# An early product moved into the first full chunk pair, a fifth buffer for cast weights in place of one for raw blocks, and token-sum stores on GpSimd's queue

## The chip, the cores and the metric

The kernel runs on one core of a Trainium2 chip. It is one program on five engines with a queue of instructions each: TensorE (PE, matrix products), VectorE (DVE), ScalarE (ACT), GpSimd (POOL) and SyncE (SP), which here only issues DMAs. An engine works through its queue in order and waits on semaphores where an instruction needs another engine's result. Copies between device memory and on-chip memory are issued from the queues of SP, POOL and, at a few places, ACT.

The metric is the device time in microseconds of one execution. Before the change it is 956.69 us, the median of 3 runs (956.43, 956.69, 957.40). The profile comes from one further execution.

## The reference

One layer on 1024 tokens of width 1024 with 16 learned meta tokens ahead. All weights and data are float32.

```python
u = rmsnorm(h, g_pre_mix[l])
z = u @ w_in[l]
q, k, v, xr, yr = jnp.split(z, split_at, axis=-1)
attn = sliding_window_attention_with_sinks(q, k, v, attn_sinks[l])
xr = causal_depthwise_conv(xr, conv_w[l], conv_b[l])
hr = rg_lru(xr, w_a[l], b_a[l], w_x[l], b_x[l], lru_lambda[l])
rec = gelu(yr) * hr
mix = concatenate([attn, rec]) @ w_out[l]
h = h + rmsnorm(mix, g_post_mix[l])
u = rmsnorm(h, g_pre_ffn[l])
f = square(relu(u @ w_ff1[l])) @ w_ff2[l]
h = h + rmsnorm(f, g_post_ffn[l])
return h[:, N_META:]
```

(The reshapes are left out.) The change mostly concerns the feed-forward part, `u @ w_ff1` (1024 to 4096, called FFN1 here) and the product with `w_ff2` (4096 to 1024, FFN2).

## The kernel before

**Precision.** A float32 operand is used as two parts. ACT casts it to a "high" part (L96), DVE subtracts that from the source and leaves a "low" part (L99); `split` issues both. A product is then three matmuls per slice, in `mm3`: high times high (L125), high times low (L126), low times high (L127). `product` calls `mm3` four times, which is twelve matmuls of 128x128 by 128x512.

**Fewer products.** Both FFN matrices and the tokens are cut into quarters, and sums and differences of quarters are multiplied, so that seven products do what eight would do plainly. FFN1 works on 16 chunks p of 256 columns of `w_ff1`. The token operands are called b11 and b21 (first half of the tokens), ot2 and ot3 (sums and differences, `t_sums`), ot1, ob22, ob21 and ot4.

- First the *early products*: `p1(p)` is a weight block times b11, `p2(p)` a weight block times b21, for chunks 0 to 3. `p2` accumulates into a bank "pt" and DVE adds the bank to block "11" (L1106). In the program text they come as p1(0), p1(1), p2(0), p2(1), the sums, p1(2), p1(3), p2(2), p2(3).
- *Stage A* (loop at L1171, p = 0 to 15): product of chunk p's first weight sum with ot2 into the bank `ya[p]`, a copy of that bank into block "12" by ACT (L1177), then `p1(p+2)`, then the product with ot3 into the same bank, and a second copy (L1181). For chunks 0 and 1 no `p1(p+2)` is left, because these were early.
- *Stage B* (`p5`, ob22, L1194 to L1214) reads one of the weight sums back from device memory.
- *Stage C* (L1299 to L1321) multiplies by ob21 and ot4. The parts of ot4 are read back from device memory, `t4_dram`, by four DMAs (L1220), and the first product on them is laid out by parts (`product_by_parts`, L1222 to L1229).
- *FFN2* (L1441 to L1468) has 7 sums i times 8 steps q. A step takes 24 matmuls.

**Weights of a chunk.** `prep_a(p)` loads two blocks of 512 KB, r0 and r1, from SP's queue. DVE builds four sums or differences in place (`combine`, L992). Two of them are split into a pair of weight buffers and one into a small pair `hl`. The last sum stays in r1 and is stored to `s_dram` from POOL's queue (L1037).

**Token sums for ot4.** `t_rest` forms them during chunks 3 to 8 of stage A, splits them, and stores four parts of 512 KB to `t4_dram` from SP's queue (L1168).

**FFN2's weights.** `fetch_2(n)` loads one or two blocks of 512 KB for step n into tags "raw" and "e" in turn; where a sum of two blocks is wanted, some steps let the second load accumulate onto the first from POOL's queue (L1261), and the others take two loads (L1264) that DVE combines in `prep_2` (L1273). Then the block is split into weight buffers (L1279).

**Buffers.** All big tiles are 4 KB per partition and come from one slab, by tag, with a fixed number of buffers each: "raw" 2, "ws" 4, "a" 16, "b" 17, "c" 8, "d" 4, "e" 3. "ws" holds cast weights (a pair takes two), "raw" and "e" hold raw blocks. In attention the key tile km sits in an "e" buffer. A new tile waits until the tile that had its buffer before has been read for the last time; this is how a buffer decides when a load or a cast can go.

**Order.** A scheduler lays the program out on the engines' queues by its own estimate of the times, so that instructions of neighbouring steps mix. `behind(name, ins)` fixes an order without a wait: ins must stand after the named instruction. `last_mm[0]` holds the name of the last matmul that `mm3` issued; `w_lows[n]` the low part of step n's weights.

Of the kernel before, what the change touches and what calls it, by code (L numbers as in the profile page):

```python
# [10 lines left out]
F32R = mybir.dt.float32r  # L11
# [5 lines left out]
P = 128  # L17
# [20 lines left out]
def hybrid_layer(  # L38
# [6 lines left out]
    nc = tc.nc  # L45
# [6 lines left out]
    ps = ctx.enter_context(tc.tile_pool(name="ps", bufs=2, space=PSUM))  # L52
    dpool = ctx.enter_context(tc.tile_pool(name="dpool", bufs=1, space=DRAM))

    bufs = {"raw": 2, "ws": 4, "a": 16, "b": 17, "c": 8, "d": 4, "e": 3}
    uid = [0]

    def slot(tag, shape, dt=F32):
        uid[0] += 1
        return slab.tile(shape, dt, tag=tag, name=f"{tag}{uid[0]}", bufs=bufs[tag])  # L60

    def pair(tag, shape):
        return slot(tag, shape, F32R), slot(tag, shape, F32R)

    def bank(tag, shape=(P, 512)):
        uid[0] += 1
        return ps.tile(list(shape), F32, tag=tag, name=f"ps_{tag}{uid[0]}")

    def f32(ap):
        return ap.bitcast(F32)  # L70
# [23 lines left out]
    def split(hi, lo, src, eng=None):  # L94
        if eng is None:
            nc.scalar.copy(hi, src)  # L96
        else:
            eng.tensor_copy(hi, src)
        low = nc.vector.tensor_tensor(lo, src, f32(hi), op=ALU.subtract).ins  # L99
        mark[0] = low.name  # L100
        return low
# [4 lines left out]
    def behind(name, *inss):  # L106
        for ins in inss:
            tc.add_manual_dep(
                ins, name,
                mybir.DependencyInfo(  # L110
                    mybir.DependencyClass.NoSync, mybir.DependencyReason.DATA
                ),
                reason="order",
            )
# [5 lines left out]
        ).ins  # L120
        return high, low

    def mm3(dst, lhs, rhs, start, stop):
        (lh, ll), (rh, rl) = lhs, rhs
        nc.tensor.matmul(dst, lh, rh, start=start, stop=False, skip_group_check=True)  # L125
        nc.tensor.matmul(dst, lh, rl, start=False, stop=False, skip_group_check=True)  # L126
        last_mm[0] = nc.tensor.matmul(  # L127
            dst, ll, rh, start=False, stop=stop, skip_group_check=True
        ).ins.name

    last_mm = [None]
# [129 lines left out]
    def project(w, pieces, sink):  # L261
        wh, wl = w
        for t0, n in pieces:
            acc = bank("acc")
            for kc in range(KC):
                uh, ul = u[kc]
                mm3(
                    acc[:, :n], (wh[:, kc, :], wl[:, kc, :]),
                    (uh[:, t0 : t0 + n], ul[:, t0 : t0 + n]),
                    kc == 0, kc == KC - 1,  # L270
                )
            sink(acc[:, :n], t0, n)
# [70 lines left out]
    def low_w(w, raw):  # L343
        chained(1, nc.vector.tensor_tensor(w[1], raw, f32(w[0]), op=ALU.subtract).ins)
# [58 lines left out]
    low_w(wv, rv)  # L403
    wq = high_w(rq)
    low_w(wq, rq)
    km = slot("e", [P, 4, 2 * P], F32R)
    nc.gpsimd.memset(f32(km[:, 0:2, 0 : P - NMETA]), 0.0)
    nc.gpsimd.memset(f32(km[:, 2:4, :]), 0.0)
    nsink = const.tile([P, 8], F32, name="nsink")
# [84 lines left out]
    for b in range(4):  # L494
# [3 lines left out]
        if b == 0:  # L498

            acc = [bank("acc"), bank("acc")]  # L500
# [11 lines left out]
            for w, (t0, n), sink, tag in (  # L512
                (wq, (16, 256), sink_q0, "o"), (wx, piece, sink_x0, "acc"),
            ):
                acc = bank(tag)
# [397 lines left out]
    t4_dram = dpool.tile([P, 2, 4, 512], F32, name="t4_dram")  # L913
# [73 lines left out]
    def w1_load(dst, b, p, a0, a1):  # L987
        c0 = 256 * p
        nc.sync.dma_start(dst, w1v[b][:, :, c0 + P * a0 : c0 + P * a1])

    def combine(dst, x0, x1, op):
        return nc.vector.tensor_tensor(dst, x0, x1, op=op).ins  # L992

    def operand(tiles):
        pairs = []
        for t_ in tiles:
            hi, lo = pair("b", [P, 2, 512])
            split(hi, lo, t_)
            pairs.append((hi, lo))
        return pairs  # L1000

    def product(acc, w, op, first):
        wh, wl = w
        for kc in range(4):
            hh, ll = op[kc // 2]
            mm3(
                acc, (wh[:, kc, :], wl[:, kc, :]), (hh[:, kc % 2, :], ll[:, kc % 2, :]),
                first and kc == 0, kc == 3,
            )

    LO, HI = slice(0, P), slice(P, 2 * P)
# [3 lines left out]
    def prep_a(p, late=None):  # L1015
        r0 = slot("raw", [P, 4, 256])
        w1_load(r0, 0, p, 0, 2)
        r1 = slot("a" if 2 <= p < 6 else "d", [P, 4, 256])
        w1_load(r1, 1, p, 0, 2)
        a11, a21, a12, a22 = r0[:, :, LO], r0[:, :, HI], r1[:, :, LO], r1[:, :, HI]  # L1020
        sums = [
            combine(a22, a21, a22, ALU.add), combine(a21, a11, a21, ALU.subtract)
        ]
        if late:
            behind(late, *sums)
        hi, lo = pair("ws", [P, 4, 256])
        if p in a11_early:
            split(hi[:, :, HI], lo[:, :, HI], a21)
            first = a11_early[p]
        else:  # L1030
            split(hi, lo, r0)
            first = hi[:, :, LO], lo[:, :, LO]
        combine(a11, a22, a11, ALU.subtract)
        hl = slot("e", [P, 2, 4, P], F32R)
        split(hl[:, 0], hl[:, 1], a11)
        combine(a12, a12, a11, ALU.subtract)
        nc.gpsimd.dma_start(s_dram[p], r1)  # L1037
        return first, (hl[:, 0], hl[:, 1]), (hi[:, :, HI], lo[:, :, HI])


    def early(b, p0, hl):
        raw = slot("raw", [P, 2, 4, P])
        for k in range(2):
            w1_load(raw[:, k], b, p0 + k, 0, 1)
        split(*hl, raw)
        return {p0 + k: (hl[0][:, k], hl[1][:, k]) for k in range(2)}

    a11_early, a12_early = {}, {}

    def fetch_b(p):  # L1050
        r1 = slot(("e", "raw")[p % 2], [P, 4, 256])
        nc.sync.dma_start(r1, s_dram[p])
        return r1
# [24 lines left out]
    def block(k, p):  # L1078
        q = p // 2
        if fb[k][q] is None:  # L1080
            fb[k][q] = slot(FTAG[k][q], [P, 2, 512])
        return fb[k][q][:, p % 2, :]
# [15 lines left out]
    def p1(p, w):  # L1098
        ya[p] = bank(("acc", "s")[p // 2 % 2])
        product(ya[p], w, b11, True)  # L1100
        nc.scalar.copy(block("11", p), ya[p])

    def p2(p, w):
        y2 = bank("pt")
        product(y2, w, b21, True)
        nc.vector.tensor_tensor(block("11", p), y2, block("11", p), op=ALU.add)  # L1106

    for t in range(8):
# [12 lines left out]
        if t == 6:  # L1121
            b21 = operand(u2f[0][2:4])
            hl = slot("b", ESH, F32R), slot("e", ESH, F32R)
# [4 lines left out]
    for p in range(2):  # L1128
        p2(p, a12_early[p])
# [10 lines left out]

    t_sums(slice(0, 3 * P))
    wa[0] = prep_a(0)
    u2_tiles(7, xns[7])
    t_sums(slice(3 * P, 4 * P))
# [1 line left out]
    for p in range(2, 4):  # L1146
        p1(p, a11_early[p])
    a12_early.update(early(1, 2, pair("a", ESH)))
    for p in range(2, 4):
        p2(p, a12_early[p])  # L1150
    ot3 = [pair("b", [P, 2, 512]) for _ in range(2)]
    for i in range(2):
        behind(urgent, split(*ot3[i], t3[i]))
# [3 lines left out]
    def t_rest(k):  # L1157
        i = k % 2
        if k < 2:
            behind(mark[0], combine(u2f[1][i], u2f[1][i], u2f[0][i], ALU.subtract))  # L1160
        elif k < 4:
            behind(mark[0], combine(t2[i], u2f[0][2 + i], t2[i], ALU.subtract))
        else:
            hl = pair("a", [P, 2, 512])
            late = mark[0]
            behind(late, split(*hl, t2[i]))
            for n in range(2):
                nc.sync.dma_start(t4_dram[:, n, 2 * i : 2 * i + 2, :], f32(hl[n]))  # L1168

    raw_b, raw_c = {}, {}  # L1170
    for p in range(16):  # L1171
        if p + 2 < 16:
            wa[p + 2] = prep_a(p + 2, None if p else urgent)
        if p >= 13:
            raw_b[p - 13] = fetch_b(p - 13)
        product(ya[p], wa[p][1], ot2, False)
        nc.scalar.copy(block("12", p), ya[p])  # L1177
        if 4 <= p + 2 < 16:
            p1(p + 2, wa[p + 2][0])
        product(ya[p], wa[p][2], ot3, False)  # L1180
        nc.scalar.copy(block("21", p), ya[p])  # L1181
        if 3 <= p < 9:
            t_rest(p - 3)

        if p == 14:
            ot1 = operand(u2f[1][0:2])
# [81 lines left out]
    def prep_2(n, tag="ws"):  # L1268
        i, q = steps[n]
        fx, wx, _ = PLAN[i]  # L1270
        raws = raw_2.pop(n)
        if len(raws) == 2:
            ins = combine(raws[0], raws[0], raws[1], wx[2])  # L1273
            if i == 6:
                behind(w_low[0], ins)
            elif i > 2:
                behind(w_lows[n - 2], ins)
        wh, wl = pair(tag, [P, 2, 512])
        w_low[0] = w_lows[n] = split(wh, wl, raws[0]).name  # L1279
        if len(fx) == 3:  # L1280
            f = slot("b", [P, 2, 512])
            combine(f, fb[fx[0]][q], fb[fx[1]][q], fx[2])
        else:
            f = fb[fx[0]][q]
        fh, fl = pair("b", [P, 2, 512])
        split(fh, fl, f)
        return fh, fl, wh, wl
# [11 lines left out]
    for n, p in enumerate(third):  # L1299
# [8 lines left out]
        if p not in a12_early:  # L1308
            y2 = bank(("acc", "s")[p % 2])
# [195 lines left out]
```

## Time and profile before

| | |
|---|---|
| median of 3 runs | 956.69 us (956.43 to 957.40) |
| the profiled execution | 955.87 us |
| its span in the trace | 954.1 us |
| granted TensorE clock, mean | 0.999 |
| early products (p1 and p2 of chunks 2 and 3 at their end) | end at about 343.5 us |
| stages A, B, C | about 343.5 to 640 us |
| FFN2 | about 640 to 948 us |

Times in the trace count from the start of the span; 1.77 us of the execution's time lie outside of it. In rows of the timeline the columns are: start, length, engine, line, operation, tile written and tiles read, sizes, number of instructions merged into the row, and in brackets the idle time before it with the instruction that ended it. Successive matmuls overlap: a row of 0.39 us is followed by the next one 0.23 us later. In the rows of a tile the three numbers are the least, median and greatest length of one instruction in ns. In the table of DMA issues the last number is the median time in us from issue to landing. PEld is the loading of weights into TensorE, SPq and POOLq are the issue of DMAs in the queues of SP and POOL.

### The profile page before, as it was taken

How to read it: one execution, taken by the hardware profiler on the slowest of the kernel's cores; microseconds unless marked ns; L12 is line 12 of the kernel's file. 1: busy time of each engine (PE TensorE's matmuls, PEld its weight loads, DVE VectorE, ACT ScalarE, POOL GpSimd, SP SyncE). 2: the span in 40 equal slices, each digit the busy share in tenths (PEclk: the TensorE clock that was granted, in tenths of full speed). 3: DMA queues.
4: the chain of work that ended last, by engine and by line, in shares of the span. 5: the costliest groups of instructions: out<-in, count | busy, mean ns of one | idle time of the engine just before them, and what ended most of it. 6: DMA issues, size and time to landing. Idle time of an engine off the chain costs nothing.

```text
span 954.1 us, 12400 instructions
## 1 busy us (share of the span) xinstructions
PE 944.0 (99%) x4728; PEld 789.3 (83%) x4728; DVE 657.8 (69%) x845; ACT 504.2 (53%) x854; POOL 125.4 (13%) x184
## 2 busy tenths in 40 slices
PE   9999999999999999999999999999999999999997
PEld 8999999877888877888888878888888888888885
DVE  6567987779866776665644465477567676779893
ACT  8537766478645554443555575663533343446441
POOL 4103564320020100000000000001111000001201
PEclk9999999999999999999999999999999999999999
DMA  8221011104225366675522354325677665537924
GB/s 273 56 67 24 23 45 46 45 23 140 81 110 177 133 220 199 198 257 162 208 100 89 111 180 129 111 88 151 164 190 172 192 210 178 197 134 196 244 45 89
DMA packets 88200, 130.21 MB, mean 136 GB/s; under 512 B 13703, under 2 KB 52631, under 8 KB 88141
## 3 DMA queue, kind: packets, MB, share of 16 engines
q1 hardware_dynamic: 79548, 106.54, 33.5%
q0 software_dynamic: 8160, 21.57, 10.8%
q10 hardware_dynamic: 432, 1.31, 0.4%
q8 instruction: 37, 0.61, 0.2%
q14 instruction: 23, 0.18, 0.1%
HBM read 109.93 MB, written 18.87 MB: 135 GB/s over the span
## 4 chain that ended last, share of the span: by engine, by line
PE 94%; DVE 2%; ACT 1%; POOL 1%; DMA 1%; issue 0%; DVEq 0%; SPq 0%; POOLq 0%; ACTq 0%
PE ps_acc L125 11%; PE ps_acc L126 11%; PE ps_acc L127 11%; PE ps_pt L125 7%; PE ps_pt L126 7%; PE ps_pt L127 7%; PE ps_s L125 6%; PE ps_s L127 6%; PE ps_s L126 6%; PE ps_o L127 5%; PE ps_o L125 5%; PE ps_o L126 5%; PE ps_o L687 1%; PE ps_acc L278 1%; DMA b<-t_dram 1%; POOL c L676 1%
## 5 line engine op out<-in xcount | busy, mean ns | idle before, releaser
L96 ACT CAST ws<-raw 128x1024 fp32r<-128x1024 f32 (+1 forms) x68 | 69.6, 1024 | 124.1 <-PE ps_o L126 49.4
L99 DVE TENSOR_TENSOR ws<-raw,ws 128x1024 fp32r<-128x1024 f32 (+1 forms) x69 | 82.4, 1194 | 61.7 <-ACT ws L96 60.6
L125 PE MATMUL ps_acc<-a,ws 128*128 128x256 f32 (+2 forms) x256 | 85.8, 335 | 0.0
L126 PE MATMUL ps_acc<-a,ws 128*128 128x256 f32 (+2 forms) x256 | 85.2, 333 | 0.0
L127 PE MATMUL ps_acc<-a,ws 128*128 128x256 f32 (+2 forms) x256 | 85.2, 333 | 0.0
L99 DVE TENSOR_TENSOR b<-b,b 128x1024 fp32r<-128x1024 f32 (+2 forms) x50 | 58.9, 1177 | 29.0 <-PE ps_o L126 20.1
L96 ACT CAST ws<-e 128x1024 fp32r<-128x1024 f32 x41 | 42.9, 1047 | 65.4 <-PE ps_o L126 42.1
L96 ACT CAST b<-b 128x1024 fp32r<-128x1024 f32 (+2 forms) x49 | 50.0, 1020 | 39.9 <-DVE b L992 34.4
L99 DVE TENSOR_TENSOR ws<-e,ws 128x1024 fp32r<-128x1024 f32 x41 | 50.1, 1222 | 22.1 <-ACT ws L96 22.1
L676 POOL TENSOR_SCALAR_AFFINE_SELECT c<-c 128x512 fp32r<-128x512 f32 x64 | 51.9, 831 | 70.4 <-ACT c L96 60.9
L125 PEld LDWEIGHTS ps_acc<-a,ws 128*128 128x128 f32 x256 | 48.3, 189 | 4.6 <-issue 0.2
L127 PEld LDWEIGHTS ps_acc<-a,ws 128*128 128x128 f32 x256 | 48.2, 188 | 4.5
L126 PEld LDWEIGHTS ps_acc<-a,ws 128*128 128x128 f32 x256 | 48.1, 188 | 4.5 <-issue 0.4
L125 PE MATMUL ps_acc<-ws,b 128*128 128x512 f32 (+1 forms) x120 | 46.2, 386 | 0.0
L127 PE MATMUL ps_acc<-ws,b 128*128 128x512 f32 (+1 forms) x120 | 46.2, 385 | 0.0
L126 PE MATMUL ps_acc<-ws,b 128*128 128x512 f32 (+1 forms) x120 | 46.1, 384 | 0.0
L125 PE MATMUL ps_pt<-ws,b 128*128 128x512 f32 x112 | 44.4, 396 | 0.0
L126 PE MATMUL ps_pt<-ws,b 128*128 128x512 f32 x112 | 44.1, 394 | 0.0
L127 PE MATMUL ps_pt<-ws,b 128*128 128x512 f32 x112 | 44.0, 393 | 0.0
L125 PE MATMUL ps_s<-ws,b 128*128 128x512 f32 x110 | 43.4, 395 | 0.0
L127 PE MATMUL ps_s<-ws,b 128*128 128x512 f32 x110 | 43.3, 394 | 0.0
L126 PE MATMUL ps_s<-ws,b 128*128 128x512 f32 x110 | 43.3, 393 | 0.0
(414 smaller groups left out, 2660.9 us busy)
## 6 DMA issues: line engine op xcount, KB each, us to landing
raw<-in_w_ff_dram SPq DMA_DIRECT2D x61, 512.0 KB, 4.8
e<-in_w_ff_dram SPq DMA_DIRECT2D x45, 512.0 KB, 3.5
d<-in_w_ff_dram SPq DMA_DIRECT2D x12, 512.0 KB
s_dram<-d POOLq DMA_DIRECT2D x12, 512.0 KB, 4.1
c<-in_x_dram SPq DMA_DIRECT2D x8, 512.0 KB, 3.4
raw<-in_w_in_dram SPq DMA_DIRECT2D x8, 512.0 KB
d<-in_x_dram SPq DMA_DIRECT2D x8, 512.0 KB, 3.3
out_dram<-raw SPq DMA_DIRECT2D x8, 512.0 KB
```

What stands on the lines that cost most here:

```text
L96: nc.scalar.copy(hi, src)
L99: low = nc.vector.tensor_tensor(lo, src, f32(hi), op=ALU.subtract).ins
L125: nc.tensor.matmul(dst, lh, rh, start=start, stop=False, skip_group_check=True)
L126: nc.tensor.matmul(dst, lh, rl, start=False, stop=False, skip_group_check=True)
L127: last_mm[0] = nc.tensor.matmul(dst, ll, rh, start=False, stop=stop, skip_group_check=True).ins.name
L278: last_mm[0] = nc.tensor.matmul(acc[:, :n], w[k // 2][:, kc, :], u[kc][k % 2][:, t0 : t0 + n], start=k == 0 and kc == 0, stop=k == last an ...
L676: nc.gpsimd.affine_select(out=p_[:, :, s], in_=f32(p_[:, :, 0]), pattern=[[0, 4], [g, P]], compare_op=op, fill=0.0, base=0, channel_multip ...
L687: nc.tensor.matmul(po[:, oc : oc + n], v, p_[:, pc : pc + n], start=first and k == 0, stop=last and k == 1, skip_group_check=True,)
```

## The change

It has five parts.

1. `p2(3)`, the last early product, is taken out of its place before ot3 and stands in stage A's loop at p = 0, between the copy at L1177 and the product with ot3. Its first matmul must stand behind the last one of the product with ot2 (`after`).
2. "ws" gets 5 buffers, "e" 2. The key tile km moves from "e" to "ws".
3. r1 of chunks 6 to 13 comes from tag "a" in place of "d".
4. The four stores to `t4_dram` are issued from POOL's queue in place of SP's.
5. In `prep_2` the combination of two blocks is held behind the low part of the step before last only at step n = 21, and no longer at all steps with i from 3 to 5.

```diff
-    bufs = {"raw": 2, "ws": 4, "a": 16, "b": 17, "c": 8, "d": 4, "e": 3}
+    bufs = {"raw": 2, "ws": 5, "a": 16, "b": 17, "c": 8, "d": 4, "e": 2}
...
-    def mm3(dst, lhs, rhs, start, stop):
+    def mm3(dst, lhs, rhs, start, stop, after=None):
         (lh, ll), (rh, rl) = lhs, rhs
-        nc.tensor.matmul(dst, lh, rh, start=start, stop=False, skip_group_check=True)
+        ins = nc.tensor.matmul(
+            dst, lh, rh, start=start, stop=False, skip_group_check=True
+        ).ins
+        if after:
+            behind(after, ins)
...
-    km = slot("e", [P, 4, 2 * P], F32R)
+    km = slot("ws", [P, 4, 2 * P], F32R)
...
-    def product(acc, w, op, first):
+    def product(acc, w, op, first, after=None):
...
-                first and kc == 0, kc == 3,
+                first and kc == 0, kc == 3, after if kc == 0 else None,
...
-        r1 = slot("a" if 2 <= p < 6 else "d", [P, 4, 256])
+        r1 = slot("a" if 2 <= p < 14 else "d", [P, 4, 256])
...
-    def p2(p, w):
+    def p2(p, w, after=None):
         y2 = bank("pt")
-        product(y2, w, b21, True)
+        product(y2, w, b21, True, after)
...
-    for p in range(2, 4):
-        p2(p, a12_early[p])
+    p2(2, a12_early[2])
     ot3 = [pair("b", [P, 2, 512]) for _ in range(2)]
...
-                nc.sync.dma_start(t4_dram[:, n, 2 * i : 2 * i + 2, :], f32(hl[n]))
+                nc.gpsimd.dma_start(t4_dram[:, n, 2 * i : 2 * i + 2, :], f32(hl[n]))
...
         nc.scalar.copy(block("12", p), ya[p])
+        if p == 0:
+            p2(3, a12_early[3], last_mm[0])
         if 4 <= p + 2 < 16:
...
             if i == 6:
                 behind(w_low[0], ins)
-            elif i > 2:
+            elif n == 21:
                 behind(w_lows[n - 2], ins)
```

## The prediction

> **What bounds the kernel now.** I read the page's head first, then what TensorE (PE) waits for, then the span cut into windows, and last the timelines around the few places where PE loses time.
>
> ```profile
> span 954.1 us, 12400 instructions
> PE 944.0 (99%) x4728; PEld 789.3 (83%) x4728; DVE 657.8 (69%) x845; ACT 504.2 (53%) x854; POOL 125.4 (13%) x184
> PE 94%; DVE 2%; ACT 1%; POOL 1%; DMA 1%; issue 0%; DVEq 0%; SPq 0%; POOLq 0%; ACTq 0%
> ...
> PE ps_acc L304 <- DVE base_e L558: 1.5, 1, 1.5
> PE ps_acc L125 <- ACT a L1177: 0.7, 1, 0.7
> PE ps_pt L1225 <- DMA b<-t_dram: 0.5, 1, 0.5
> PE ps_o L687 <- POOL c L676: 0.3, 1, 0.3
> ```
>
> The last four lines are all the waits of PE (total us, times, longest). PE is busy for 99% of the span, and the chain that ended last is PE for 94% of it. So a step that does not remove matmuls can only win back PE's gaps. Where they lie, by windows (columns: window and length, then busy us and instruction count of PE, weight loads, DVE, ACT, POOL; clock, DMA share, GB/s):
>
> ```profile
> 340.00:366.00 26.00, 25.32 (x107) 19.42 (x106) 19.23 (x29) 11.81 (x19) 1.61 (x3) 1.00 0.61 203
> 366.00:460.00 94.00, 94.00 (x406) 76.18 (x406) 57.73 (x75) 39.75 (x60) 6.40 (x12) 1.00 0.64 210
> ...
> 560.00:650.00 90.00, 89.50 (x387) 72.18 (x386) 54.62 (x59) 55.80 (x57) 0.00 (x0) 1.00 0.35 113
> 700.00:900.00 200.00, 200.00 (x864) 162.18 (x863) 147.72 (x140) 85.48 (x105) 14.50 (x13) 1.00 0.65 189
> ```
>
> After 340 us PE misses 0.68 us at the first full chunk pair (26.00 − 25.32) and 0.50 us behind 560. From 366 to 460 and from 700 to 900 it misses nothing. The tail behind the last matmuls is not touched by the change. Attention waits 0.3 us (L687). So the pool of gains inside the changed stages is 0.68 + 0.50 + 0.3 = 1.5 us, plus matmuls that run slowly right after a stall, which busy time hides. A loss has no such ceiling: every engine except PE has room, and what it delays shows once the room is used up.
>
> **The moved early product.** PE's timeline, first to last:
>
> ```profile
> 337.96 0.39 PE L125 MATMUL ps_pt<-b,a 128*128 128x512 f32 x1
> ...
> 343.28 0.39 PE L127 MATMUL ps_pt<-b,a 128*128 128x512 f32 x1
> 343.50 0.39 PE L125 MATMUL ps_acc<-b,e 128*128 128x512 f32 x1
> ...
> 346.04 0.40 PE L127 MATMUL ps_acc<-b,e 128*128 128x512 f32 x1
> 347.11 0.50 PE L125 MATMUL ps_acc<-b,ws 128*128 128x512 f32 x1 [0.68 <-ACT a L1177]
> 347.44 0.39 PE L126 MATMUL ps_acc<-b,ws 128*128 128x512 f32 x1
> ...
> 350.04 0.50 PE L125 MATMUL ps_acc<-b,e 128*128 128x512 f32 x1
> ...
> 351.13 0.48 PE L127 MATMUL ps_acc<-b,e 128*128 128x512 f32 x1
> ```
>
> The first two rows are the ends of 24 matmuls: p2(2) and p2(3), twelve each, spaced (343.28 − 337.96) / 23 = 0.231 us. Behind them come product ot2 of chunk 0 (343.50 to 346.04), a copy of its bank on ACT, and product ot3 into the same bank. That last one must wait: at 0.231 us it would have started at 346.27 and started at 347.11, so 0.84 us are lost, and 0.10 us more by the first spacing of 0.33 us (347.11 to 347.44). The change puts p2(3), 12 × 0.231 = 2.77 us of work, into that hole. What has to be ready earlier:
>
> ```profile
> 346.47 0.58 ACT L1177 COPY a<-ps_acc 128x512 f32<-128x512 f32 x1 [5.23 <-PE ps_acc L127]
> ...
> 340.02 0.76 DVE L99 TENSOR_TENSOR b<-a,b 128x256 fp32r<-128x256 f32 x2 [0.63 <-ACT b L96]
> 341.38 0.69 DVE L1106 TENSOR_TENSOR b<-ps_pt,b 128x512 f32<-128x512 f32 x1 [0.60 <-PE ps_pt L127]
> ...
> 350.37 1.28 DVE L99 TENSOR_TENSOR e<-raw,e 128x512 fp32r<-128x512 f32 x2
> ```
>
> Product ot2 can start at 343.50 − 2.77 = 340.73. Of its two late operand parts (340.02, x2) the second now stands behind the eviction L1106 of p2(2) in DVE's order. That eviction itself comes earlier, since in the old order two matmuls of p2(3) stood inside p2(2) and now none does: 341.38 − 2 × 0.231 = 340.92, plus 0.61 (the pitch to its next instruction) = 341.53, and the part, half of the row's 0.76, is there by 341.9. PE wants it at its eighth matmul, 340.73 + 7 × 0.231 = 342.35: hidden by 0.4. The copy then starts at 343.7 and ends by 344.3, under p2(3), which runs until 346.27. So product ot3 starts there, 0.84 us earlier.
>
> What is late next is the second wait in the rows above: product ot2 of chunk 1 needs the low part of its weights (350.37, x2; the first half ends at about 351.06), and PE got to it at 351.13. In the new DVE order that part comes 0.46 earlier with the eviction of p2(2), 0.61 earlier because one combine of chunk 2 now stands behind it, and 0.37 later by the operand part now ahead: 0.70 in all, done at 350.36. PE would be there after 16 matmuls, 346.27 + 3.70 = 349.97, so it waits 0.4 us here and goes on at 350.43. Gain 0.7 us: of the 0.84, the low part gives the rest back. Ends: 0.1 (the low part isn't earlier at all) and 1.2 (every gap here closes).
>
> The load of chunk 3 is released by that same low part:
>
> ```profile
> 351.08 1.57 SPq L989 DMA_DIRECT2D raw<-in_w_ff_dram  x2
> ...
> 357.07 0.69 DVE L992 TENSOR_TENSOR a<-raw,a 128x512 f32<-128x512 f32 x1 [4.81 <-DMA raw<-in_w_ff_dram]
> ```
>
> DVE idles 4.81 us for it, while PE, with the products of chunks 1 and 2 in front of it, runs on without a wait. An issue 0.7 us earlier keeps the distance; no new stall. A larger gain upstream would meet this load, which is why 1.2 is an end and not a forecast.
>
> **Blocks of stage A and stores.** A block of r1 for chunks 6 to 13 now takes an "a" buffer in place of "d", so r1 loads of chunks 14 and 15 and some others come forward in SP's queue, ahead of a raw block. The four stores of the token sums leave SP:
>
> ```profile
> 397.58 0.34 SPq L1168 DMA_DIRECT2D t_dram<-a  x1
> ...
> 401.04 0.53 POOL L1037 DMA_DIRECT2D s_dram<-d  x1 [9.62 <-DVE d L992]
> ...
> s_dram<-d POOLq DMA_DIRECT2D x12, 512.0 KB, 4.1
> t_dram<-a SPq DMA_DIRECT2D x4, 512.0 KB, 4.1
> ```
>
> SP's queue gives back 4 × 0.34 us of issue; POOL takes 4 × 0.53 us where it idles 9.62 us ahead of a store. The data is read at 552 us, over 130 us later. That time covers the move; without it, it would cost one landing, 4.1 us. Stage A misses 0.00 of 94 us from 366 to 460, so the early loads can only harm; one 512 KB block ahead in the queue is worth 1.6 us (below), and a loss would need two of them on a block that is due at once. I take 0, with 0 and +1.6 as bounds. Of the Trainium skill, "SBUF — State Buffer" (the box on DVE blocking a DMA, in its section on the doors) speaks against this step: a DMA from GpSimd's queue has its descriptors written by GpSimd, which DVE can lock out while it runs certain two-port operations. No row here shows it: both kinds of store land in 4.1 us. By the rule the sum would grow only through what stands behind the stores; that is the last rival below.
>
> **The reload of the sums (ot4).** In SP's queue two high halves stand ahead of two low ones. With the third "e" buffer gone, one 512 KB block of stage C, which used to be loaded ahead of all four, is released later and stands between the high and the low halves.
>
> ```profile
> 552.22 2.73 SPq L1220 DMA_DIRECT2D b<-t_dram  x4
> ...
> b<-t_dram SPq DMA_DIRECT2D x4, 512.0 KB, 5.3
> ...
> 559.21 2.58 PE L1225 MATMUL ps_pt<-b,ws 128*128 128x512 f32 x10
> 562.29 0.73 PE L1225 MATMUL ps_pt<-b,ws 128*128 128x512 f32 x2 [0.50 <-DMA b<-t_dram]
> 562.86 0.39 PE L125 MATMUL ps_s<-b,ws 128*128 128x512 f32 x1
> ...
> 554.01 8.23 DMA b<-t_dram
> ```
>
> Twelve matmuls from 559.21 would end at 561.98; the next one started at 562.86, so 0.87 us are lost to the last low half, issued at 554.01 and landed at 562.24. The first low half was there in time: matmuls 9 and 10 use it from 559.21 + 8 × 0.231 = 561.06. A block's turn in the queue: if the first reload took the median 5.3 us it landed at 557.5, and the other three by 562.24, so 1.6 us each. In the new order of PE two matmuls of another product stand ahead and one more between, so the first low half is wanted 3 × 0.231 later, at 561.75; with one block more ahead it lands at 561.06 + 1.6 = 562.66 at the latest, a wait of up to 0.9 us. I take the middle between that and a landing half a block earlier, 0.55, and 0.1 of slow start. The second low half now has 16 matmuls, 3.7 us, behind the first and is covered. Net 0.87 − 0.65 = 0.2 us gained; ends: all of 0.87, and, at 203 GB/s as in the window from 340 (2.6 us for 512 KB), a loss of 1.9 + 0.1 − 0.87 = 1.1 us.
>
> **FFN2 with two raw "e" buffers and five for weights.** Here PE is full, and only a loss is possible. The tile view of the fourth and fifth product sums of FFN2, 775 to 862 us, with the landing of "e" there and, one line on, from 640 to 800 us:
>
> ```profile
> L1264 SPq DMA_DIRECT2D raw<-in_w_ff_dram x14: 367/368/368, 776.6 to 854.6; - x14
> ...
> L1264 SPq DMA_DIRECT2D e<-in_w_ff_dram x14: 367/368/368, 778.9 to 860.5; - x14
> ...
> DMA to landing us min/median/max: 3.1/3.6/4.2
> ...
> DMA to landing us min/median/max: 3.1/5.5/7.3
> ...
> 775.00:862.00 87.00, 87.00 (x376) 70.48 (x375) 61.77 (x58) 36.17 (x45) 0.00 (x0) 1.00 0.50 170
> ```
>
> "raw" already has two buffers and is loaded as often as "e" (14 each), and PE misses 0.00 of 87 us. A third "e" buffer is thus not what keeps PE full. A step is 24 × 0.231 = 5.55 us. With two buffers a block has two steps, 11.1 us, less landing (4.2 at worst), combine, cast and low (about 1.2 + 1.05 + 1.2): over 3 us are left. A fifth weight buffer lets a cast go one release earlier, and dropping the fixed place of the combine (except at step 21) lets DVE take it sooner. I take 0, bounds 0 and the rival's price. In attention the key tile km goes from "e" to a weight buffer, which leaves four there as before, and POOL, DVE and ACT are reordered; only 0.3 us of waiting can go, and as much can come: 0 ± 0.5.
>
> **Sum.** 0.7 + 0.2 = 0.9 us less. The profiled execution took 955.87 us (span 954.1 and 1.77 around it), so it would take 954.97; the median of the runs shown is 956.69, 0.82 above it, and I predict on the median: 955.8 us.
>
> **Rivals.**
> 1. All gaps close: 0.84 + 0.10 and 0.3 between 350.04 and 351.13 (1.09 us for four matmuls of 0.93, and slow spacings behind), 0.87 at the reload, attention's 0.3: 2.4 us, 954.3. For it: each has one named cause that the change touches. Against: DVE's order puts the low part of chunk 1 at 350.36 at best.
> 2. The wait only moves: the low part stays at 351.06, stage A gains 0.1, the reload loses 1.1 us, an early block in stage A up to 1.6: 957.7, at most 959.3. For it: DVE is 74% busy in that window (19.23 of 26.00), and a block goes ahead of the late reload. Against: DVE's new order, counted above.
> 3. Slower: two "e" buffers in FFN2. The combine stands in DVE's one queue and now, unordered, may wait there for a block that lands late, with the low parts of the step before behind it. It decides from the point where landing exceeds the slack of about 3 us + 4.2 = 7 us; the other windows reach 7.3 (640 to 800), where accumulating loads run beside. Price 0.5 to 1 us in each of 12 pairs of steps: 6 to 12 us, 962.7 to 968.7. Against: "raw" lives with two buffers today.
> 4. Stores on POOL hold up the s_dram stores behind them, and their r1 blocks come free late: at most four times DVE's longest instruction here, 4 × 1.28 = 5.1 us less POOL's idle 9.62: about 0, and 961.8 if nothing covered it.
>
> **How the numbers follow.** Forecast 0.47, rivals 0.17, 0.20, 0.14 and 0.02. A change of 0.2% (1.9 us, about what can be told from none) is 954.8 to 958.6. Faster: most of rival 1 and a tail of the forecast, 0.19. Slower: rivals 3 and 4 and the end of rival 2, 0.20. Same: 0.61. The forecast's own range is 954.6 to 957.0 (0.7 and 0.2 at their ends, less attention's 0.5 either way); the range over the cases is 954.0 to 960.0, which leaves out rival 3's price and the best end of rival 1.
>
> **What would show it.** Right: PE's wait on L1177 is gone; the first ot3 product starts about 0.8 us earlier, and 0.4 us of wait show up on chunk 1's low part (DVE e L99); no new PE wait from 366 to 550; the wait at L1225 is under 0.5 us; PE stays full from 700 to 900. Wrong: a PE wait on the low part of chunk 1's or 2's weights of 0.7 us or more, a wait on t_dram over 1 us, or a busy time of PE under 199 of 200 us in FFN2 with waits on DVE ws L99; a changed span before 340 us would show that attention, which I priced at nothing, carries the difference.

## The result, and the profile after

The changed kernel takes 961.43 us, the median of 7 runs (960.57 to 965.12); the kernel before takes 956.72 us over the 7 runs beside it (956.43 to 959.1). The ratio is 1.0056 with a 95% interval of 1.0038 to 1.0074. The forecast was 955.8 with a range up to 960.0: the kernel became slower, by 4.7 us, and the range missed it.

The profiled execution of the changed kernel took 964.96 us, the second longest of the seven, so its losses are shown at their larger size. A second profile comes with the experiments (961.92 us). The head of the page:

```profile
span 963.3 us, 12447 instructions
PE 946.5 (98%) x4728; PEld 790.3 (82%) x4728; DVE 655.7 (68%) x845; ACT 505.9 (53%) x854; POOL 128.3 (13%) x188
PE 82%; DVE 5%; issue 4%; DMA 4%; ACT 3%; POOL 1%; SPq 0%; DVEq 0%; POOLq 0%; ACTq 0%
```

The same number of matmuls, 2.5 us more busy time, and 9.2 us more span. PE's part of the chain that ended last fell from 94% to 82%: other engines now set the pace somewhere. All waits of PE (us in total, times, longest):

```profile
PE ps_acc L130 <- DVE ws L99: 5.4, 5, 3.3
PE ps_acc L308 <- DVE base_e L562: 1.5, 1, 1.5
PE ps_acc L125 <- ACT ws L96: 1.3, 2, 0.7
PE ps_o L357 <- DVE d L248: 0.6, 1, 0.6
PE ps_o L691 <- POOL c L680: 0.3, 1, 0.3
PE ps_pt L130 <- DVE a L99: 0.2, 1, 0.2
```

The two waits of before that the prediction worked on, on L1177 and on t_dram, are both gone. In their place stand 6.7 us on cast weights, "ws". The windows tell the stage (same columns as before):

```profile
340.00:366.00 26.00, 25.93 (x112) 20.61 (x111) 18.97 (x30) 13.06 (x21) 1.61 (x3) 1.00 0.64 208
366.00:460.00 94.00, 94.00 (x408) 76.20 (x407) 59.23 (x76) 40.78 (x60) 8.55 (x16) 1.00 0.64 209
560.00:650.00 90.00, 90.00 (x390) 72.98 (x390) 53.95 (x59) 57.05 (x58) 0.00 (x0) 1.00 0.37 113
700.00:900.00 200.00, 195.06 (x830) 156.61 (x829) 142.71 (x135) 79.75 (x100) 13.21 (x12) 0.99 0.65 182
900.00:963.30 63.30, 54.23 (x278) 45.12 (x277) 42.81 (x53) 23.34 (x41) 7.52 (x7) 0.96 0.51 107
```

and the end of the kernel before:

```profile
900.00:954.10 54.10, 47.03 (x251) 40.13 (x249) 37.28 (x48) 19.44 (x38) 5.11 (x5) 0.98 0.42 86
```

Up to 650 us the change does what was forecast, and better: PE misses 0.07 us at the first chunk pair where it missed 0.68, and nothing behind 560. Then 4.94 us are missing between 700 and 900, where nothing was missing (this is the sign of being wrong that the prediction named, under 199 of 200 us), and at the end 9.07 us where 7.07 were missing. Both places are in FFN2.

To see where time is won and lost in each run, the table counts matmuls in order of their starts, and gives by how many us the distance between two of these counts differs from the kernel before's profile (positive: longer). Counts are 50, 2050, 2250, 3000, 3100, 3850, 4000, 4400 and 4700, which in the kernel before start at 11, 335, 382, 556, 580, 754, 789, 882 and 943 us. All experiments stand in it.

```text
                              to 11  335   382   556   580   754   789   882   943 | sum
after                           0.7   0.0  -1.1  -0.1  -0.9   0.0   7.7   0.1   2.6 | 9.0
e1_order_back                   1.0  -0.1  -1.1  -0.1  -0.9   0.0   0.0   0.1   2.1 | 1.1
e2_buffers_back                 0.5   0.0  -1.1   0.4  -0.4   0.5   0.0   1.6   0.0 | 1.5
e3_product_alone                0.7   0.0  -1.0   3.9  -0.4   0.0   0.0   0.0   0.0 | 3.2
e4_buffers_alone                1.0  -0.1   0.4   0.4  -0.9   0.0   0.0   0.1   1.7 | 2.7
e5_parts_1_3_4                  0.8   0.0  -1.1   0.6  -0.8   0.0   0.0   0.0   0.0 | -0.6
e6_order_back_stores_late       0.8   0.0  -1.1  -0.1  -0.9   0.0   0.0   0.1   0.0 | -1.1
e7_no_accumulation              1.3   0.0  -1.1  -0.1  -0.9   0.0   0.0   0.1   3.1 | 2.5
e8_order_alone                  0.6   0.0   0.1   3.9   0.4   0.0   0.0   1.7   0.0 | 6.6
e9_one_combine_held             0.6   0.2  -1.1  -0.1  -0.4   0.0   1.1   0.1   2.1 | 2.4
e10_product_and_r1              0.7   0.0  -1.1   1.6  -0.7   0.0   0.0   0.0   0.0 | 0.4
e11_changed_again               1.0   0.2  -1.1  -0.1  -0.9   0.0   3.6   0.1   3.1 | 5.9
```

The first column is not the change: all twelve other profiles, even those with nothing altered there, started 0.5 to 1.3 us slower than the one of before. It is part of the sum in the last column, and is left out of what follows. Each row is one execution. The columns 382 and 580 are the two gains, 789 and 943 the two losses.

**The loss at 754 to 789 us.** DVE's timeline in the changed kernel:

```profile
770.65 1.22 DVE L996 TENSOR_TENSOR raw<-raw,e 128x1024 f32<-128x1024 f32 x1 [5.62 <-DMA e<-in_w_ff_dram]
771.79 1.22 DVE L99 TENSOR_TENSOR ws<-raw,ws 128x1024 fp32r<-128x1024 f32 x1
```

DVE sits for 5.62 us in front of a combine (L996, step 26 of FFN2) whose second block has not landed. Behind it stands the low part of step 24 (the next row), and PE started with that at 773.06 after 3.27 us of waiting. The low part's own source was combined at 751.30, and ACT had cast its high part by 761.7:

```profile
760.62 1.04 ACT L96 CAST ws<-raw 128x1024 fp32r<-128x1024 f32 x1
```

Of the 7.7 us, 4.9 are waits of PE: 0.72 and 0.76 at 757 and 758, 3.27 at 773 and 0.19 at 781. Another 1.6 us come from a stretch behind the long wait in which the matmuls run slowly although PE is busy. The window shows a granted clock of 0.51:

```profile
774.00:777.40 3.40, 3.40 (x10) 2.63 (x9) 0.74 (x2) 0.00 (x0) 0.00 (x0) 0.51 0.96 351
```

From 774.21 to 777.20 successive matmuls started 0.43 us apart in place of 0.23. The rest is slow spacing just behind the waits. The second profile of the changed kernel (e11 below) has no such stretch, and its loss here is 3.6 us.

### The profile page after: what moved, and what is told of

Read it like the earlier page. It is cut to its first block, busy times and chain, and to the rows that moved or that the text cites. A ratio compares the mean times of both kernels' runs of the same rounds, so it can differ in the third digit from the quotient of the medians.

```text
span 963.3 us, 12447 instructions
## 1 busy us (share of the span) xinstructions
PE 946.5 (98%) x4728; PEld 790.3 (82%) x4728; DVE 655.7 (68%) x845; ACT 505.9 (53%) x854; POOL 128.3 (13%) x188
## 4 chain that ended last, share of the span: by engine, by line
PE 82%; DVE 5%; issue 4%; DMA 4%; ACT 3%; POOL 1%; SPq 0%; DVEq 0%; POOLq 0%; ACTq 0%
PE ps_acc L130 10%; PE ps_acc L131 10%; PE ps_acc L125 9%; PE ps_s L131 6%; PE ps_s L130 6%; PE ps_s L125 6%; PE ps_pt L130 5%; PE ps_pt L131 5%; PE ps_pt L125 5%; PE ps_o L130 5%; PE ps_o L125 5%; PE ps_o L131 5%; ACT c L82 1%; DMA b<-in_w_ff_dram 1%; PE ps_o L691 1%
```

## The experiments

Two theories stood at first. *Order*: the combine, no longer held behind an earlier low part, blocks DVE's queue. *Buffers*: two "e" buffers instead of three make the loads late, whatever DVE's order. Each run has its own runs of the kernel before beside it; ratios are to these.

### The rule for the combine put back (e1)

```diff
 # on the changed kernel
-            elif n == 21:
+            elif i > 2:
```

> The changed kernel with the old rule for the combine (held behind the low part of the step before last in all steps with i from 3 to 5). Order theory (DVE idles at a combine whose block lands late, and a low part that was ready stands behind it): the 3.27 us wait at 773 us goes and with it most of the loss, 957 to 958.5 us. Buffer theory (four raw buffers in place of five make the loads of FFN2 late wherever DVE takes them): PE still waits 3 us or more between 740 and 790 us, 960 us or more.

Measured: 957.47 against 957.41 us, ratio 1.0001 (0.9991 to 1.0011). The loss at 754 to 789 is gone altogether, 7.7 to 0.0. What is left is the one at the end. This is as the order theory had it. Yet the loads are as late as in the changed kernel, as ACT's waits from 690 to 760 us show: in the kernel before,

```profile
ACT ws L96 <- PE ps_o L126: 26.3, 13, 3.6
```

in the changed kernel,

```profile
ACT ws L96 <- DMA raw<-in_w_ff_dram: 26.4, 5, 11.1
ACT ws L96 <- DMA e<-in_w_ff_dram: 12.7, 3, 4.5
```

and in this run:

```profile
ACT ws L96 <- DMA raw<-in_w_ff_dram: 17.8, 5, 4.9
ACT ws L96 <- DMA e<-in_w_ff_dram: 16.6, 4, 4.5
```

Before, a cast waited for PE to free a weight buffer: the block was there, and PE set the pace. Now 8 or 9 casts wait for the block itself. The buffer theory is right about the loads, but with the combine held, late loads cost PE nothing here. The rule also changes the last two accumulating loads on GpSimd's queue: here the block that is needed first is loaded first (raw at 740.48, e at 748.09), in the changed kernel it is loaded last (e at 741.40, raw at 750.24). There its cast ran only at 755.88, after the wait of 11.1 us above, and the two PE waits of 0.7 us at 757 and 758 followed. This exchange alone was not run.

### The buffers put back (e2)

```diff
 # on the changed kernel
-    bufs = {"raw": 2, "ws": 5, "a": 16, "b": 17, "c": 8, "d": 4, "e": 2}
+    bufs = {"raw": 2, "ws": 4, "a": 16, "b": 17, "c": 8, "d": 4, "e": 3}
-    km = slot("ws", [P, 4, 2 * P], F32R)
+    km = slot("e", [P, 4, 2 * P], F32R)
```

> The changed kernel with 4 weight buffers, 3 buffers e and the key tile in e, all else as changed (the combine is free but for step 21). Buffer theory: loads are early again, no PE wait over 0.2 us in FFN2, 955 to 956 us. Order theory: the combines still stand ahead of low parts, PE waits of 2 us or more in FFN2, 959 us or more.

Measured: 958.52 us, ratio 1.0010 (0.9997 to 1.0023): neither number. The 7.7 are gone here too, no cast waits for a DMA from 690 to 760 us, and the loss at the end is gone (0.0). But 1.6 us are lost between 789 and 882, with PE waits of 0.66 and 0.35 us on low parts: a free combine still costs something with three "e" buffers. So the big loss shows only with both parts of the change at once.

### The free combine alone (e8)

```diff
 # on the kernel before
-            elif i > 2:
+            elif n == 21:
```

> The kernel before with the combine no longer held (but at step 21) and nothing else: three buffers e. If the lost time needs both a free combine and late loads: PE waits in FFN2 of at most 1 us in all, ratio 1.000 to 1.001. If the free combine does it alone: 3 us or more of PE waits between 740 and 860 us, ratio 1.003 or more.

Measured: 959.57 against 957.23 us, ratio 1.0030 (1.0017 to 1.0042), a miss for the first expectation by its ratio, although the waits it named (at most 1 us in FFN2) came as expected: 0.58 and 0.17 us. In FFN2 it lost 1.7 us, the same place and size as in e2, and no more. The profiled execution was the slowest of its six (962.88 us). It also lost 3.9 us in stage A, where all queues stand in the order of the kernel before; the rows:

```profile
450.11 0.50 PE L125 MATMUL ps_s<-b,ws 128*128 128x512 f32 x1 [1.28 <-ACT ws L96]
451.37 0.50 PE L127 MATMUL ps_s<-b,ws 128*128 128x512 f32 x1 [0.52 <-DVE ws L99]
```

Behind them the granted clock was 0.50 from 452.3 to 455.7. So stage A of the kernel before stands close to a stall that shows in some executions, and the median of e8 is 3.3 us below the one that shows it. It turns up again in e3.

### The buffers alone (e4)

```diff
 # on the kernel before
-    bufs = {"raw": 2, "ws": 4, "a": 16, "b": 17, "c": 8, "d": 4, "e": 3}
+    bufs = {"raw": 2, "ws": 5, "a": 16, "b": 17, "c": 8, "d": 4, "e": 2}
-    km = slot("e", [P, 4, 2 * P], F32R)
+    km = slot("ws", [P, 4, 2 * P], F32R)
```

> The kernel before with 5 weight buffers, 2 buffers e and the key tile in ws, nothing else; the combine is held as before. Buffer theory: 960 us or more, PE waits in FFN2 on cast weights, and casts that wait for DMA at every step from 700 us. Order theory: casts wait for DMA but PE hardly does, 956 to 957.5 us.

Measured: 960.16 against 957.41 us, ratio 1.0028 (1.0018 to 1.0038). The time is that of the buffer theory, its place is not: in FFN2 nothing is lost up to 882 us, then 1.7 us at the end. The same run has the whole gain of 0.9 us at the reload of ot4, with nothing else of the change; e5 and e10 below have most of it without the buffers.

### One combine held (e9)

```diff
 # on the changed kernel
-            elif n == 21:
+            elif n in (21, 26):
```

> The changed kernel with one more combine held: that of step 26, behind the low part of step 24. In DVE's queue two neighbours change places there, and the same once more a step on; GpSimd's queue stays as changed. Head-of-line theory: the 3.27 us wait at 773 us goes, while the waits of 0.7 us at 757 and 758 us (an accumulating load behind another one, on GpSimd) stay; 2 to 3 us less than the changed kernel. Buffer theory: the low part is late anyhow, 3 us of waits move to the next step.

Measured: 957.77 against 957.53 us, ratio 1.0003 (0.9991 to 1.0015), where the changed kernel stood at 1.0056. The medians lie 3.7 us apart, where 2 to 3 were expected. The loss at 754 to 789 falls from 7.7 (3.6 in the second profile) to 1.1, of which 0.66 us is a wait at 757.70; of the two waits that were to stay, this one did. DVE now:

```profile
764.37 1.22 DVE L99 TENSOR_TENSOR ws<-raw,ws 128x1024 fp32r<-128x1024 f32 x1
768.98 1.23 DVE L996 TENSOR_TENSOR raw<-raw,e 128x1024 f32<-128x1024 f32 x1 [3.39 <-DMA e<-in_w_ff_dram]
```

The low part goes first, at 764.37. DVE still waits 3.39 us for the same block, but nobody stands behind it. Beside this exchange the order changes only at the next combine, one matmul of PE and two loads of SP's queue, so the wait of an instruction at the head of DVE's queue is shown as the cause of the 3.27 us.

### The accumulating loads left out (e7)

```diff
 # on the changed kernel, in fetch_2
             ):
-                nc.gpsimd.dma_start(raws[0], w2v[q, a, b], accum_op=ADD)
+                if i == 6:
+                    nc.gpsimd.dma_start(raws[0], w2v[q, a, b], accum_op=ADD)
                 break
```

> The changed kernel without the second block of the 12 accumulated weight sums of FFN2's second and third sums (left out, so these weights are one block instead of two). If the accumulating loads, one at a time on GpSimd's queue, are what makes the loads late that DVE later waits for at 745 to 780 us: casts between 700 and 745 us no longer wait for DMA, and the 4.9 us of PE waits from 750 to 785 us shrink below 1 us. If two buffers of e are too few for the combined pairs by themselves: the 3.27 us wait at the first pairs stays.

Measured in one execution: 958.57 us. No cast waits for a DMA from 690 to 760 us, and the loss at 754 to 789 is 0.0 although buffers and combine are those of the changed kernel. So it is the accumulated blocks that make the loads late. (This kernel leaves out 12 transfers of 512 KB as well as their place on the queue; the run can't tell the two apart.) How, the changed kernel shows; first POOL's queue, then ACT's:

```profile
704.26 1.22 POOL L1266 DMA_DIRECT2D e<-in_w_ff_dram  x1 [6.88 <-DVE b L996]
710.34 1.20 POOL L1266 DMA_DIRECT2D raw<-in_w_ff_dram  x1 [4.86 <-DVE b L996]
716.36 1.22 POOL L1266 DMA_DIRECT2D e<-in_w_ff_dram  x1 [4.83 <-issue]
```

```profile
704.03 1.05 ACT L96 CAST ws<-raw 128x1024 fp32r<-128x1024 f32 x1 [4.56 <-DMA raw<-in_w_ff_dram]
710.10 1.05 ACT L96 CAST ws<-e 128x1024 fp32r<-128x1024 f32 x1 [4.08 <-DMA e<-in_w_ff_dram]
716.13 1.05 ACT L96 CAST ws<-raw 128x1024 fp32r<-128x1024 f32 x1 [4.03 <-DMA raw<-in_w_ff_dram]
```

Each row of ACT is a cast released by the landing of an accumulating load; 0.23 us later POOL issues the next one. They go one at a time, 6.0 us apart, while a step of PE takes 5.55. A block that is accumulated so holds its buffer through two transfers in turn. For one such block: its first load was issued at 692.08, its accumulating load at 696.18, its cast ran at 704.03 and its low part ended at 707.20: 15 us.

```profile
692.08 0.37 SPq L1269 DMA_DIRECT2D raw<-in_w_ff_dram  x1
...
696.18 1.20 POOL L1266 DMA_DIRECT2D raw<-in_w_ff_dram  x1 [11.15 <-DVE ws L99]
...
705.98 1.23 DVE L99 TENSOR_TENSOR ws<-raw,ws 128x1024 fp32r<-128x1024 f32 x1 [2.02 <-PE ps_o L130]
```

These sums take 20 buffers in 16 steps (12 accumulated steps, and 4 with two blocks). With the step at 5.55 us that is one buffer every 4.44 us, so four buffers may be held 17.8 us each, and five 22.2. At 15 us and more per block, four are just at their limit and five were not. That the lead of the kernel before came with its five raw buffers is in e2, which exchanges both tags at once; the counting of hold times itself is an estimate from these rows.

### The moved product alone (e3), and with the r1 blocks (e10)

e3 is the kernel before with the five lines of the diff that move `p2(3)`. e10 has one line more:

```diff
-        r1 = slot("a" if 2 <= p < 6 else "d", [P, 4, 256])
+        r1 = slot("a" if 2 <= p < 14 else "d", [P, 4, 256])
```

> The kernel before with the early product moved and nothing else. Both theories: 0.7 us less in the stretch from 340 to 366 us, the wait on the copy L1177 gone, 956.0 us.

> The kernel before with the early product moved and the r1 blocks of chunks 6 to 13 in a; the token sums stay on SP's queue. If the loss at 424 to 452 us of the product alone comes from r1's blocks in d (loaded anew only when their store has landed): no PE wait from 366 to 500 us, ratio 0.999. If it comes from the four stores in SP's queue: PE waits of 2 us or more there, ratio 1.002.

Measured: e3 959.79 against 957.41 us, ratio 1.0026 (1.0017 to 1.0035), slower, where both theories had 956.0. The gain at 335 to 382 is there (1.0), but stage A gives back 3.9. The chain ahead of PE's waits of 1.32 us at 450.62 and 0.52 us at 451.88:

```profile
437.47 5.12 DMA s_dram<-d
...
442.61 5.26 DMA d<-in_w_ff_dram
```

The store of one r1 block takes 5.12 us to land; only then its "d" buffer may be loaded anew, which takes 5.26 us, and DVE, ACT and PE wait in turn. That is the stall that e8 showed without the moved product (there 5.01 and 5.57 us). e10 took 957.72 against 957.53 us, ratio 1.0005 (0.9996 to 1.0015). It has nothing of this at 450, but waits of 0.49 and 0.52 us stay at 423 to 424 us: one place cured, the other not, so neither half of the expectation holds alone.

### Product, r1 blocks and stores, old buffers and rule (e5)

The changed kernel with the edits of e1 and e2 together.

> The changed kernel with both the old buffers and the old rule for the combine: what is left of the change is the moved product, the r1 blocks in a, and the stores on GpSimd's queue. Theory (the loss comes from the two parts taken out; the r1 blocks in a cure the 3 us that the moved product alone loses at 424 to 452 us): 1.1 us less at 340 to 370 us, no PE wait from 366 to 550, none in FFN2, the wait on t_dram stays; ratio to before 0.999. Rival (the loss at 424 to 452 comes from the earlier PE itself, whatever r1's buffer): PE waits of 2 us or more there, ratio 1.002 or more.

Measured: 956.03 against 957.23 us, ratio 0.9994 (0.9980 to 1.0007), not to be told from the kernel before. With the stores on POOL's queue stage A's column falls from 1.6 (e10) to 0.6, with one PE wait of 0.33 us at 440. The intervals of e5 and e10 overlap, so this last step rests on one profile each. FFN2 loses nothing anywhere. The wait on t_dram did not stay as expected: the reload gains 0.8 here.

### The early output stores behind two accumulating loads (e6)

What still costs 2.1 us in e1 lies at the last weight sum of FFN2. POOL's queue in the changed kernel:

```profile
869.84 0.91 POOL L1345 DMA_DIRECT2D out_dram<-a  x1 [118.38 <-ACT sd L82]
876.02 0.86 POOL L1345 DMA_DIRECT2D out_dram<-a  x1 [5.28 <-ACT a L1332]
883.90 0.89 POOL L1345 DMA_DIRECT2D out_dram<-a  x1 [7.01 <-DVE a L1341]
885.19 0.87 POOL L1345 DMA_DIRECT2D out_dram<-a  x1 [0.41 <-issue]
894.38 1.21 POOL L1266 DMA_DIRECT2D b<-in_w_ff_dram  x1 [8.32 <-issue]
```

Four output stores of `finish_early` stand ahead of the first accumulating load, which is then issued at 894.38, when the third store, which took 10.2 us, had landed. The expectation below has each of these waiting for the one before; for the loads that is so, but the last two stores were issued 1.29 us apart. In the kernel before two of the stores stood behind two loads:

```profile
871.92 0.86 POOL L1340 DMA_DIRECT2D out_dram<-a  x1 [5.05 <-DVE a L1336]
875.18 1.21 POOL L1261 DMA_DIRECT2D b<-in_w_ff_dram  x1 [2.39 <-PE ps_o L127]
884.56 1.23 POOL L1261 DMA_DIRECT2D b<-in_w_ff_dram  x1 [8.16 <-DVE ws L99]
885.29 1.43 POOL L1340 DMA_DIRECT2D out_dram<-a  x1
```

In the changed kernel the cast of the first load's block ended 10.3 us after that load was issued, and PE waited for it:

```profile
903.63 1.05 ACT L96 CAST ws<-b 128x1024 fp32r<-128x1024 f32 x1 [7.11 <-DMA b<-in_w_ff_dram]
```

```diff
 # on e1
+    accs_6 = {}
...
-                nc.gpsimd.dma_start(raws[0], w2v[q, a, b], accum_op=ADD)
+                accs_6[n] = nc.gpsimd.dma_start(
+                    raws[0], w2v[q, a, b], accum_op=ADD
+                ).ins.name
...
-        nc.gpsimd.dma_start(out[t * P : (t + 1) * P, :], o, accum_op=ALU.add)
+        store = nc.gpsimd.dma_start(
+            out[t * P : (t + 1) * P, :], o, accum_op=ALU.add
+        ).ins
+        if j >= 2:
+            behind(accs_6[50], store)
```

> The changed kernel with the old rule for the combine, and the third and fourth early output stores placed behind the second accumulating load of the last sum in GpSimd's queue, as in the kernel before. Queue theory (the 1.3 us of waits and 2 us of shift from 897 to 924 us come from these two stores ahead of the accumulating loads, each waiting for the one before to land): no PE wait over 0.2 us after 880 us, 2 us less than without, ratio to before 0.998. Buffer theory (SP issues the first block of these pairs 13 us later, and that is what counts): the waits from 897 us on stay, ratio 1.000.

Measured: 955.39 against 957.23 us, ratio 0.9982 (0.9973 to 0.9991): faster than both kernels. The last loss is 0.0, and all waits of PE that are left lie before FFN1:

```profile
PE ps_acc L308 <- DVE base_e L562: 1.5, 1, 1.5
PE ps_o L357 <- DVE d L248: 0.5, 1, 0.5
PE ps_o L691 <- POOL c L680: 0.3, 1, 0.3
PE ps_pt L130 <- DVE a L99: 0.2, 1, 0.2
PE ps_s L357 <- DVE d L248: 0.2, 1, 0.2
```

Against e1, every other queue has the same order of instructions, so the order on GpSimd's queue was the cause. The buffers alone (e4) also put the stores ahead and lost 1.7; with the old buffers (e2, e5) two of them stood behind, and nothing was lost.

### The changed kernel again (e11)

> The changed kernel once more, for a second profile. If the combine ahead of the low part is the cause in every execution: a PE wait on a low part of 1 us or more between 755 and 790 us, and DVE idle for DMA e ahead of a combine at the same place. If the profile of the changed kernel was a chance event: no wait over 0.5 us there.

Measured in one execution: 961.92 us. PE waits 1.42 and 1.59 us on low parts at 769.57 and 777.26, and DVE ahead of it:

```profile
767.15 1.23 DVE L996 TENSOR_TENSOR raw<-raw,e 128x1024 f32<-128x1024 f32 x1 [4.10 <-DMA e<-in_w_ff_dram]
768.30 1.22 DVE L99 TENSOR_TENSOR ws<-raw,ws 128x1024 fp32r<-128x1024 f32 x1
```

Same place, same pair of instructions, 4.10 us instead of 5.62. How late the block lands differs from one execution to the next, and with it the loss (3.6 against 7.7); the stretch of low granted clock, 1.6 us of the 7.7, is missing here. That fits the spread of the changed kernel's runs, 4.6 us.

## Why the prediction was wrong

**The moved product: right, mis-sized.** The wait on L1177 went, and product ot3 followed p2(3) without a gap, 0.82 us earlier against the matmuls ahead of p2(2), as worked out (0.84). On chunk 1's low part PE was held up by 0.24 us, where 0.4 was worked out. Three slow spacings of the kernel before, from 362 to 365 us, went as well and gave 0.27 us that the forecast did not have. Gain 1.0 to 1.1 us in every run that has it, for 0.7.

**What the product needs in stage A: missed.** The prediction took 0 for the r1 blocks and the stores because stage A lost nothing before. They are in fact what keeps the gain: without the r1 blocks in "a" the store and reload of a "d" buffer, 10.4 us in turn, cost up to 3.9 us (e3, e8, one profile each), and without the stores on POOL 1 us more was lost in the one profile of e10 than in that of e5. In the changed kernel they did cost nothing, so the number stood for the wrong reason: the "bound" that early loads can only harm had the sign wrong. The last rival, stores that hold up GpSimd's queue in stage A, didn't occur: DVE was 63% busy from 366 to 460 us (59.23 of 94.00), and PE missed 0.00. The rule of the Trainium skill ("SBUF — State Buffer", section "SBUF: two separate sides", the box on DVE blocking a DMA) had no cost here. That is no test of it: all of DVE's instructions in this stretch are of the kind TENSOR_TENSOR, and the one operation that the box names is another, `tensor_copy`.

**The reload: mis-sized.** The whole 0.87 us came, for the 0.2 taken; its upper end was this. The step had PE's new order right: in the changed kernel the last low half is wanted 3.7 us after the first (which is the seventh matmul of the first row, at 561.22), and PE does not wait for it.

```profile
559.83 2.03 PE L1230 MATMUL ps_pt<-b,ws 128*128 128x512 f32 x8
...
564.94 0.62 PE L1230 MATMUL ps_pt<-b,ws 128*128 128x512 f32 x2
```

The delay of 0.65 us that it set against this, by the block that now stands between the high and the low halves, was 0 in all runs with the new buffers but e9, which waited 0.18 us on the first low half and gained 0.4. With the old buffers (e2, e3, e5, e8, e10) PE keeps the order of the kernel before and comes to the last low half 7.5 us after its issue. What is lost then depends on its landing: 8.23 us after the issue in the kernel before, and PE could go on 7.5 us after it in e5, 7.6 in e10, 7.9 in e2 and e3, and 8.7 in e8. So the gain of e5 and e10 there is a quicker landing in that execution, and not shown to be the change.

**FFN2 with two "e" buffers: the step that failed.** It took 0 for FFN2, and the two profiles of the changed kernel lost 3.6 and 7.7 us at 754 to 789, and 3.1 and 2.6 at the end. It read "A third 'e' buffer is thus not what keeps PE full", from the window 775 to 862 us. That window holds only weight sums made of two plain loads, which landed in 3.6 us. The second and third sums before it, about 684 to 773 us, are the accumulated ones, where 12 of 16 steps need two transfers in turn, and the second goes one at a time on GpSimd's queue. The median of 5.5 us for 640 to 800 was shown and did not enter the slack, and it covered only one of the two transfers. The slack of "over 3 us" was a slack of other steps.

**The free combine: priced with the wrong sign.** The prediction said that dropping its place "lets DVE take it sooner". An instruction that comes sooner in an in-order queue also waits sooner, with all that stands behind it: 5.62 us at one place. Its rival 3 described just this and gave the point from which it decides; it was given 0.14 and left out of the range because "raw" lives with two buffers. Rival 3's price, 0.5 to 1 us in each of 12 pairs, was wrong in form: waits of up to 3.3 us at the first two pairs, where the lateness of the accumulated sums arrives, and then nothing. That DVE catches up there because the plain loads are shorter is a reading and was not tested.

**The end of FFN2: not seen.** "The tail behind the last matmuls is not touched" overlooked the part of FFN2 just ahead of it. GpSimd's order of the output stores moved with the buffers, and 1.7 to 3.1 us were lost in the runs that have it.

The sum over the parts, from the columns: −1.1 − 0.9 + 7.7 + 2.6 = 8.3 us more in the first profile and −1.1 − 0.9 + 3.6 + 3.1 = 4.7 in the second; the medians differ by 4.7. Also, the upper end of the forecast's own range, 957.0, does not follow from its terms: 956.69 − 0.1 + 1.1 is 957.7.

What stays open: why the reload of a low half lands up to 1.2 us sooner or later in runs whose order there is the same, and why the first 11 us differ by up to 1.3 us between executions of the same instructions.

## What to carry to other kernels

A buffer's slack has to be read in the stage where a tile holds it longest, over all its transfers in turn, and not where the same tag is seen most often. A busy share of 100% says nothing on how far the loads are ahead: whether casts wait for PE or for DMA does, and here casts waited for DMA from 690 us on, while PE lost nothing before 757. Before freeing an order on an in-order engine, ask what the freed instruction waits for, and which work that is ready would then stand behind it.

## What the runs showed of the hardware

Accumulating loads of 512 KB from GpSimd's queue went one at a time: the next was issued 0.23 us after the cast that the former had released (710.34 after 710.10, 716.36 after 716.13), although its own first load had been issued 11 to 15 us before and the kernel's text sets no wait of the one for the other. Why is not shown: the program is built with `dynamic_dma_scratch_size=1024`, which no run altered. Other DMAs of the same queue did overlap. An accumulating load followed an output store after 3.26 us (875.18 after 871.92 above), and that store took 7.7 us to land. Two plain stores were issued 0.60 us apart in the kernel before:

```profile
350.15 0.55 POOL L1037 DMA_DIRECT2D s_dram<-d  x1 [16.76 <-DVE d L992]
350.75 0.53 POOL L1037 DMA_DIRECT2D s_dram<-a  x1
```

A granted clock of about 0.5 for 3.4 us followed a PE wait of 3.27 us in the changed kernel (774.0 to 777.4) and waits of 1.28 and 0.52 us in e8 (452.3 to 455.7). It did not follow waits of 1.32 and 0.52 us at the same place in e3. So such a stretch can add to a loss, and these traces don't tell when.
